# Turning the second group's frames on VectorE instead of TensorE, with K chunks by channel quarters

## The chip, the core and the metric

One core of a Trainium2 chip runs the whole kernel. The metric is the device time of one execution in microseconds (us). The engines are named as in the profile: PE is TensorE (matmuls; PEld its weight loads), DVE is VectorE, ACT is ScalarE, POOL is GpSimd and SP is the engine that issues most of the DMAs.

## What is computed

One layer of a streaming encoder for 2048 prompt frames and 32 sample frames of 1024 channels, all in fp32:

```python
hn = rmsnorm(h, g_mix)
proj = hn @ w_in                                  # 1024 -> 6 x 512
hA, bA, cA, zA, vB, zB = split(proj)              # 512 channels each
u = cA * hA
yA = bA * (causal conv, width 3, of u + bias) * silu(zA)
yB = (trailing means of vB over 2/4/8/16 frames, minus vB, @ pool_w, * scale) * silu(zB)
h = h + concat[yA, yB] @ w_out
h = h + (p @ w_ple) * sigmoid(rmsnorm(h, g_ple) @ w_ple_gate)
y = rmsnorm(h, g_final)                           # and the last u and v rows as states
```

The sum over the 1024 input channels of `hn @ w_in` may be taken in any order, if frames and weights use the same one. The change is about that order.

## The kernel before

**Exact products from parts.** An fp32 operand is held as two tiles, hi and lo. `split` (L81 and L84) makes them: ACT casts the hi part (L81) and VectorE subtracts it from the source to get lo (L84). A product runs as three passes over the pairs (hi·hi, hi·lo, lo·hi), each of four matmuls of 128x128 by 128x512 for a half of K, so 12 matmuls (`half_product`, L646).

**Seven products in place of eight.** The 2048 frames form four blocks of 512. `GROUPS` pairs them: group 0 has blocks 0 and 1, group 1 has blocks 2 and 3. The two blocks of a group and the two halves of the 1024 channels make a 2x2 matrix of frames, and two kinds of columns of w_in with the two halves make a 2x2 matrix of weights. One `pair` of projections takes seven products of combinations: of frames 11, 21, 22 and T1 to T4 (differences and sums of the four quarters of the matrix), of weights 11, 12, 22 and S1 to S4 (tiles `w_..._S`). `pair_weights` (L597) loads two raw weight tiles of 128x1024 (`raw_..a`, `raw_..b`) and builds the sums on VectorE (L606, L618). The results of a pair gather in three PSUM tiles x, y and z, which ACT and VectorE drain (L983, L986).

**Units.** A `Unit` (gi, j) is a group and a quarter j of 128 columns of each of the six projections. It runs three pairs, named zbv (zb and v), ch (c and h) and zab (za and b), between them the pooling matmuls `pm` (L870 to L872), the drain of pm (L874) and the convolution (four scalar-tensor-tensor steps on VectorE, L1103). The first unit of group 0 runs `plain`, without the seven products for the first ones. The order of units is group 0 with j from 0 to 3, then group 1.

**Frames of group 0.** Eight tiles of 128 frames x 1024 channels are loaded (`x_load`), their sum of squares is taken on ACT, rstd on POOL, and VectorE normalises them in place: block 0 with two 512-column instructions a tile (L700), block 1 with one of 1024 (L477). PE turns each 128x128 block through the identity (`turn`, L484, PSUM tiles `pt`) so that channels lie on partitions. `second_block` makes the combinations with block 1 during the plain unit. Of the seven pieces six fit; T4 is written to DRAM (`p_d["T4"]`) in four columns and read back as one piece of 2 MB into tile `B_T` (L941).

**Frames of group 1.** While group 0's units 1 to 3 run, the steps of `frame_sums` (L498) are called in small portions between the products (`aside`, at a pace of 13 steps in 18 calls). They go by columns: column c is the tile c of block 2 and the tile c of block 3, in the order 3, 0, 1, 2. A column is loaded (two DMAs of 512 KB), normalised on VectorE (L477), turned by PE (16 transposes into `pt_g`), combined on VectorE (`f_g`, L509), and each of its seven pieces is split into a staged tile and written to DRAM by POOL (`to_memory`, L546; names such as `11_1_3` for piece 11 of group 1, column 3, and `T` for the T's). At the end of group 0 `load_group(1)` (L556) loads seven pieces of 2 MB on POOL's queue (L560) and two raw weight tiles behind them.

**Buffers.** Frames, staged tiles and some weights share a pool of four tiles (`xin`), raw weights one of three (`raws`), split weights one of six. A staged tile is free again when its write has landed.

**Order.** Each engine has its own queue, and a scheduler fixes the order in it when the program is built; `tc.keep_in_program_order` (`in_turn`, `later`) pins single instructions to their place in the source. An engine never overtakes its own queue: an instruction that waits holds all behind it.

Of the kernel before, what the change touches and what calls it, by code (L numbers as in the profile page):

```python
# [36 lines left out]
def trunk(ctx, tc, x_p, x_s, c_conv, c_pool, p_p, p_s, g_mix, w_in, conv_w, conv_b, pool_w,  # L37
# [361 lines left out]
    with ExitStack() as s1:  # L399
# [78 lines left out]

        def turn(x, half, name, get=tbank, later=False):
# [92 lines left out]

        def raw_weight(kind, j, name, ring=raw_ring, queue=nc.sync):
# [4 lines left out]
            raw_loads.append(queue.dma_start(t, w_in[:, col:col + P].rearrange("(k p) n -> p k n", p=P)))  # L578
# [18 lines left out]
        def pair_weights(gi, ka, kb, j, name, ring, s_ring, ring_b, pin):  # L597
# [9 lines left out]
            if (ka, j) in kept:  # L607
# [5 lines left out]
                raw_loads.append(nc.sync.dma_start(rb[:, KH:], w_in[NH:, col:col + P].rearrange("(k p) n -> p k n", p=P)))  # L613
# [75 lines left out]
        B0 = {}  # L689
        ahead0 = [x_load(f"0_{c}", x_rows(0, c)) for c in range(4)]  # L690
# [3 lines left out]

        def first_normal(x):

            xt, m, r = x
            for half in range(2):
                h = xt[:m, half * NH:half * NH + NH]
                in_turn(nc.vector.scalar_tensor_tensor(h, h, r[:m], pg[half][:m], op0=ALU.mult, op1=ALU.mult))  # L700
# [76 lines left out]
        def second_block():  # L777

            spans = [(c, slice(c * P, c * P + P)) for c in range(4)]
            xs = []  # L780
            for c in range(4):
                x = x_stat(x_load(f"1_{c}", x_rows(1, c)))
                normal(x)
                xs.append(x)
                yield
            whole = []
            for c, cs in spans:
                x = xs[c]

                turned = x[0].rearrange("p (k t) -> p k t", k=KC)  # L790
# [7 lines left out]
            for c, cs in spans:  # L798
# [12 lines left out]
                to_memory(p_d["T4"], f"T4_0_{c}", t4, c * P)  # L811
                yield

        second = second_block()
# [21 lines left out]
        class Unit:  # L836
# [65 lines left out]
            def plain(self):  # L902
# [11 lines left out]

                wz, wv = weights("zb", j, f"zb{tag}"), weights("v", j, f"v{tag}")
# [24 lines left out]
                B0["T4"] = piece_of(seventh("B0_T4"), 0)  # L940
                nc.gpsimd.dma_start(B0["T4"].bitcast(F32), p_d["T4"])  # L941
# [261 lines left out]
        def next_columns(*cs):  # L1203

            ahead[cs[0]] = columns_in(1, cs[0])
# [636 lines left out]
```

## Time and profile before

| | |
|---|---|
| median of 3 runs | 919.31 us (918.29 to 919.38) |
| the profiled execution | 917.26 us |
| span of its trace | 915.5 us (1.76 us lie around it) |
| granted TensorE clock | 0.999 |
| PE busy | 895.3 us (98%), 4174 matmuls |
| VectorE busy | 702.6 us (77%) |
| ACT busy | 460.3 us (50%) |
| POOL busy | 151.6 us (17%) |

The units of group 0 end at about 277 us, the projections of group 1 run after them, and the output projection, gate and final norm fill the rest. A timeline row has the start, the duration, the engine, the line, the operation with output<-input, and in brackets the idle time before it with what ended it. A row of a line's summary has minimum, median and maximum duration in ns, and the first and the last start.

### The profile page before, as it was taken

How to read it: one execution, taken by the hardware profiler on the slowest of the kernel's cores; microseconds unless marked ns; L12 is line 12 of the kernel's file. 1: busy time of each engine (PE TensorE's matmuls, PEld its weight loads, DVE VectorE, ACT ScalarE, POOL GpSimd, SP SyncE). 2: the span in 40 equal slices, each digit the busy share in tenths (PEclk: the TensorE clock that was granted, in tenths of full speed). 3: DMA queues.
4: the chain of work that ended last, by engine and by line, in shares of the span. 5: the costliest groups of instructions: out<-in, count | busy, mean ns of one | idle time of the engine just before them, and what ended most of it. 6: DMA issues, size and time to landing. Idle time of an engine off the chain costs nothing.

```text
span 915.5 us, 12179 instructions
## 1 busy us (share of the span) xinstructions
PE 895.3 (98%) x4174; PEld 722.7 (79%) x4174; DVE 702.6 (77%) x1158; ACT 460.3 (50%) x834; POOL 151.6 (17%) x291
## 2 busy tenths in 40 slices
PE   8999999999999999999999999999999999999996
PEld 6787888878888877877778887888888788778885
DVE  6897899697894597856667679965576978897885
ACT  7743555555444344533344366544344865565554
POOL 2210121222122104100000020121111211120002
PEclk9999999999999999999999999999999999999999
DMA  8165386749499857577746485787677875575554
GB/s 275 53 186 184 115 239 182 219 147 301 122 313 427 244 161 228 191 231 247 244 132 215 146 310 206 259 235 273 226 258 291 287 256 173 184 234 187 183 187 171
DMA packets 113307, 199.56 MB, mean 218 GB/s; under 512 B 13190, under 2 KB 70062, under 8 KB 112221
## 3 DMA queue, kind: packets, MB, share of 16 engines
q1 hardware_dynamic: 91309, 124.72, 42.3%
q0 software_dynamic: 19488, 69.67, 22.5%
q10 hardware_dynamic: 2448, 4.39, 1.3%
q8 instruction: 33, 0.54, 0.2%
q14 instruction: 29, 0.24, 0.1%
HBM read 133.06 MB, written 65.67 MB: 217 GB/s over the span
## 4 chain that ended last, share of the span: by engine, by line
PE 65%; DMA 7%; issue 5%; DVE 2%; ACT 1%; POOL 1%; SPq 0%; POOLq 0%; DVEq 0%; ACTq 0%
PE x_g L185 9%; PE x_o L185 9%; PE x_zab L646 5%; PE z_g L185 5%; PE e L109 4%; PE x_zbv L646 4%; PE x_ch L646 4%; PE z_o L185 4%; DMA raw_zab_0b<-in_w_in_dram 4%; PE z_zab L646 2%; PE y_g L185 2%; PE y_o L185 2%; PE z_ch L646 2%; PE z_zbv L646 2%; DMA B<-p_d 2%
## 5 line engine op out<-in xcount | busy, mean ns | idle before, releaser
L646 PE MATMUL x_zab<-B,w_zab_S 128*128 128x512 f32 x192 | 46.9, 392 | 0.6 <-ACT V L983 0.4
L185 PE MATMUL z_o<-wo,y_S 128*128 128x512 f32 x192 | 47.4, 389 | 0.0
L185 PE MATMUL z_g<-wg,g_S 128*128 128x512 f32 x192 | 46.8, 391 | 0.0
L646 PE MATMUL z_zab<-B,w_zab_S 128*128 128x512 f32 x192 | 46.7, 390 | 0.0
L185 PE MATMUL x_o<-wo_T,y_S 128*128 128x512 f32 x192 | 46.1, 389 | 0.0
L185 PE MATMUL x_o<-wo,y 128*128 128x512 f32 x192 | 45.2, 389 | 0.0
L646 PEld LDWEIGHTS x_zab<-B,w_zab_S 128*128 128x128 f32 x192 | 35.7, 188 | 9.6 <-ACT V L983 0.8
L185 PEld LDWEIGHTS x_o<-wo,y 128*128 128x128 f32 x192 | 36.1, 188 | 7.7
L646 PEld LDWEIGHTS z_zab<-B,w_zab_S 128*128 128x128 f32 x192 | 35.8, 188 | 7.8 <-DVE w_zab_S L84 0.3
L185 PEld LDWEIGHTS z_o<-wo,y_S 128*128 128x128 f32 x192 | 36.0, 188 | 7.5
L646 PE MATMUL x_ch<-B,w_ch_S 128*128 128x512 f32 x168 | 41.9, 392 | 0.0
L185 PEld LDWEIGHTS x_o<-wo_T,y_S 128*128 128x128 f32 x192 | 36.0, 188 | 7.4
L646 PE MATMUL z_ch<-B,w_ch_S 128*128 128x512 f32 x168 | 40.5, 390 | 1.4 <-ACT U L983 1.4
L185 PEld LDWEIGHTS z_g<-wg,g_S 128*128 128x128 f32 x192 | 35.8, 188 | 7.5 <-ACT c_g L1566 0.2
L646 PE MATMUL x_zbv<-B,w_zbv_S 128*128 128x512 f32 x168 | 40.8, 392 | 0.6 <-ACT zs L983 0.6
L646 PE MATMUL z_zbv<-B,w_zbv_S 128*128 128x512 f32 x168 | 40.4, 390 | 0.0
L646 PEld LDWEIGHTS z_ch<-B,w_ch_S 128*128 128x128 f32 x168 | 31.5, 188 | 8.3 <-ACT U L983 1.8
L646 PEld LDWEIGHTS x_zbv<-B,w_zbv_S 128*128 128x128 f32 x168 | 31.3, 188 | 8.3 <-ACT zs L983 1.0
L646 PEld LDWEIGHTS x_ch<-B,w_ch_S 128*128 128x128 f32 x168 | 31.3, 188 | 7.3 <-issue 0.4
L646 PEld LDWEIGHTS z_zbv<-B,w_zbv_S 128*128 128x128 f32 x168 | 31.5, 188 | 6.5
L81 ACT CAST y_S<-y_fS 128x512 fp32r<-128x512 f32 x28 | 17.0, 620 | 27.2 <-PE x_o L185 11.5
L1316 DVE TENSOR_TENSOR c_o<-x_o,x 128x512 f32<-128x512 f32 x14 | 9.7, 690 | 21.9 <-PE x_o L185 21.8
(550 smaller groups left out, 2289.4 us busy)
## 6 DMA issues: line engine op xcount, KB each, us to landing
wn<-in_w_in_dram SPq DMA_DIRECT2D x24, 512.0 KB, 5.3
p_dT<-T POOLq DMA_DIRECT2D x16, 512.0 KB, 5.4
y<-y_d SPq DMA_DIRECT2D x16, 512.0 KB, 6.5
e<-e_d SPq DMA_DIRECT2D x15, 512.0 KB, 4.5
x<-in_x_prompt_dram SPq DMA_DIRECT2D x14, 512.0 KB, 5.2
B<-p_d POOLq DMA_DIRECT2D x3, 2048.0 KB, 15.7
B<-p_dT POOLq DMA_DIRECT2D x3, 2048.0 KB, 21.6
h_d<-x SPq DMA_DIRECT2D x12, 512.0 KB, 7.2
```

Source lines behind the costliest of these rows:

```text
L81: ins = nc.scalar.copy(hi, src)
L109: nc.tensor.matmul(ps, pps[:, a, k], wp[k][b][:, cs], start=k + q == 0, stop=k == 1 and q == 2)
L185: nc.tensor.matmul(ps[:n], lhs[:, k, a, :n], w[b][:, k], start=start and k + q == 0, stop=k == KH - 1 and q == 2, skip_group_check=True)
L646: nc.tensor.matmul(ps, lhs[:, k, x], b[:, k, y], start=start and k + q == 0, stop=stop and k == KH - 1 and q == 2, skip_group_check=True)
L1316: add = lambda o, a, b: nc.vector.tensor_tensor(o, a, b, op=ALU.add)
```

## The change

It takes the K dimension in another order, the same for frames and weights: chunk k, partition q·32 + r is channel q·256 + k·32 + r (before, channel k·128 + partition). In that order a turn needs only the transpose of 32x32 blocks, and VectorE has an instruction for that.

- **Frames of group 1**: a tile is loaded with four DMAs, each a quarter of the channels onto 32 partitions, so that VectorE's transpose of 32x32 blocks (128x1024 at once, in place) gives the turned tile. PE's 64 transposes, their PSUM tiles and two copies by ACT a column are gone. The sum of squares comes in eight squares of 128x256 a column and is put together across the four partition quarters on POOL; the normalisation is eight instructions of 128x256. The combinations are made in place in the two loaded tiles, which therefore hold two of the four tiles of `xin` until T4 is split; the seven pieces share the other two as staged tiles.
- **Weights of w_in**: every raw tile is loaded in that order, with four DMAs of 32 partitions in place of one of 128.
- **Frames of group 0**: still turned by PE. The normalisation writes a copy with the channels in the new order, as four instructions of 128x8x32 a tile.
- **T4 of group 0**: only the columns 0 to 2 go through DRAM (1.5 MB are read back, once column 2 is written), and the last column is split directly into `B_T`.

The core of the diff:

```diff
+        def normal_into(t, x, in_order=False, g=None):
+            xt, n, r = x
+            for q in range(4):
+                cs = slice(q * 2 * P, q * 2 * P + 2 * P)
+                o, h = t[:, :D].rearrange("p (k q c) -> p q k c", k=KC, q=4)[:, q], xt[:, cs].rearrange("p (k c) -> p k c", k=KC)
+                by = (g[q // 2][:, q % 2 * 2 * P:(q % 2 + 1) * 2 * P] if g else g_bc[:, cs]).rearrange("p (k c) -> p k c", k=KC)
+                ins = nc.vector.scalar_tensor_tensor(o, h, r, by, op0=ALU.mult, op1=ALU.mult)
+                if in_order:
+                    in_turn(ins)
+            return t, n, r
...
-            return [x_load(f"{tb}_{c}", x_rows(tb, c), queue) for tb in GROUPS[g]]
-        def four(xs, tag):
-            for half in range(2):
-                yield [turn(x, half, f"pt_{tag}_{i}_{half}", get=bank if half else tbank, later=True) for i, x in enumerate(xs)]
-        def frame_sums(xs, tag, dst):
-            xs = [x_stat(x, True) for x in xs]
+            xs = []
+            for tb in GROUPS[g]:
+                t = ring4(xin, f"xt_{tb}_{c}")
+                rows = x_rows(tb, c).rearrange("(g p) (q c) -> q p g c", p=32, q=4)
+                for q in range(4):
+                    queue.dma_start(t[q * 32:q * 32 + 32].rearrange("p (g c) -> p g c", g=4), rows[q])
+                xs.append(t)
+            return xs
+        def frame_sums(xs, tag, dst, norms):
+            for _ in range(3):
+                yield
+            g_q, part = norms[:, :2 * P], lambda i: norms[:, 2 * P + i * 8:2 * P + i * 8 + 8]
+            ssq, tot, ms, rr, other = (part(i) for i in range(5))
+            quarter = lambda i: slice(i * 32, i * 32 + 32)
+            for b, x in enumerate(xs):
+                for g in range(4):
+                    i = b * 4 + g
+                    tc.keep_in_program_order(nc.scalar.activation(junk[:, :2 * P], x[:, g * 2 * P:(g + 1) * 2 * P], AF.Square,
+                                                                  accum_out=ssq[:, i:i + 1]))
+                yield
+            first = quarter(0)
+            for q in range(1, 4):
+                nc.gpsimd.tensor_copy(other[first], ssq[quarter(q)])
+                nc.gpsimd.tensor_tensor(tot[first], other[first], (tot if q > 1 else ssq)[first], op=ALU.add)
+            nc.gpsimd.tensor_scalar(ms[first], tot[first], scalar1=1.0 / D, scalar2=EPS, op0=ALU.mult, op1=ALU.add)
+            nc.gpsimd.tensor_tensor(rr[first], ms[first], nhalf[first].to_broadcast([32, 8]), op=ALU.pow)
+            for q in range(1, 4):
+                nc.gpsimd.tensor_copy(rr[quarter(q)], rr[first])
+            for b, x in enumerate(xs):
+                for g in range(4):
+                    h = x[:, g * 2 * P:(g + 1) * 2 * P]
+                    nc.vector.scalar_tensor_tensor(h, h, rr[:, b * 4 + g:b * 4 + g + 1], g_q, op0=ALU.mult, op1=ALU.mult)
             yield
             for x in xs:
-                normal(x)
-                yield
-            f12, f1, f21 = (ftile(f"{c}_{tag}") for c in ("f12", "f1", "f21"))
+                nc.vector.transpose(x, x)
+            yield
+            u = [x.rearrange("p (g k t) -> p k g t", g=4, k=KC) for x in xs]
+            (p11, p21), (p12, p22) = ((v[:, :KH], v[:, KH:]) for v in u)
             sub = lambda o, x, y: nc.vector.tensor_tensor(o, x, y, op=ALU.subtract)
-            steps = four(xs, tag)
-            p11, p12 = next(steps)
-            nc.scalar.copy(f12, p12)
-            sub(f1, f12, p11)
             dst("11", p11)
-            yield
-            dst("T1", f1)
-            yield
-            p21, p22 = next(steps)
-            nc.scalar.copy(f21, p21)
-            sub(f1, p22, f1)
-            sub(f12, p22, f12)
+            sub(p11, p12, p11)
+            yield
+            dst("T1", p11)
+            sub(p11, p22, p11)
             yield
             dst("21", p21)
+            sub(p21, p21, p11)
+            yield
+            dst("T2", p11)
+            sub(p12, p22, p12)
             yield
             dst("22", p22)
-            yield
-            dst("T2", f1)
-            sub(f21, f21, f1)
-            yield
-            dst("T3", f12)
-            yield
-            dst("T4", f21)
-            yield
+            dst("T3", p12)
+            yield
+            dst("T4", p21)
...
             t = staged(name)
-            put(t, src, later)
+            whole = (lambda v: v.rearrange("p k (g t) -> p k g t", g=4)) if len(src.shape) == 4 else lambda v: v
+            split(whole(t[:, :, 0]), whole(t[:, :, 1]), src, later=later)
             nc.gpsimd.dma_start(mem[:, :, :, at:at + P], t.bitcast(F32))
...
+        def load_chunks(t, col, queue=nc.sync, ks=slice(0, KC)):
+            rows = w_in[:, col:col + P].rearrange("(q k c) n -> q c k n", q=4, k=KC)
+            for q in range(4):
+                raw_loads.append(queue.dma_start(t[q * 32:q * 32 + 32], rows[q][:, ks]))
         def raw_weight(kind, j, name, ring=raw_ring, queue=nc.sync):
             if name in raw_ahead:
                 return raw_ahead.pop(name)
             t = ring(f"raw_{name}")
             col = cols[kind] * WA + j * P
-            raw_loads.append(queue.dma_start(t, w_in[:, col:col + P].rearrange("(k p) n -> p k n", p=P)))
+            load_chunks(t, col, queue)
             return t
...
         def first_tile(c):
-            first_normal(first_x[c])
-            turned_x[c] = [turn(first_x[c], half, f"pt0_{c}_{half}", bank) for half in range(2)]
+            x = normal_into(room0 if c == 0 else ahead0[c - 1][0], first_x[c], True, pg)
+            turned_x[c] = [turn(x, half, f"pt0_{c}_{half}", bank) for half in range(2)]
...
                 op(t4, t4, part("21", 1), ALU.add)
-                to_memory(p_d["T4"], f"T4_0_{c}", t4, c * P)
+                if c < 3:
+                    to_memory(p_d["T4"], f"T4_0_{c}", t4, c * P)
+                else:
+                    B0["T4"] = piece_of(seventh("B0_T4"), 0)
+                    nc.gpsimd.dma_start(B0["T4"][:, :, :, :c * P].bitcast(F32), p_d["T4"][:, :, :, :c * P])
+                    put(B0["T4"][:, :, :, cs], t4)
                 yield
...
         def next_columns(*cs):
             ahead[cs[0]] = columns_in(1, cs[0])
+            norms = ftile("norms").rearrange("p k n -> p (k n)")
+            for q in range(4):
+                nc.gpsimd.dma_start(norms[q * 32:q * 32 + 32, :2 * P], g_mix[:, q * 2 * P:(q + 1) * 2 * P].partition_broadcast(32))
             for c, after in zip(cs, cs[1:] + (None,)):
                 dst = lambda q, src: to_memory(p_d[q], f"{q}_1_{c}", src, c * P, True)
-                for i, _ in enumerate(frame_sums(ahead.pop(c), f"g1_{c}", dst)):
-                    if i == 10 and after is not None:
-                        ahead[after] = columns_in(1, after, nc.gpsimd)
-                    yield
+                yield from frame_sums(ahead.pop(c), f"g1_{c}", dst, norms)
+                if after is not None:
+                    ahead[after] = columns_in(1, after, nc.gpsimd)
                 yield
```

More of the change, by code (lines that the diff above doesn't have):

```diff
@@ L612, in pair_weights @@
                 nc.sync.dma_start(rb[:, :KH], k3)
-                raw_loads.append(nc.sync.dma_start(rb[:, KH:], w_in[NH:, col:col + P].rearrange("(k p) n -> p k n", p=P)))
+                load_chunks(rb[:, KH:], col, ks=slice(KH, KC))
                 s3, a22 = rb[:, :KH], rb[:, KH:]
@@ L689, in trunk @@
         B0 = {}
+        room0 = bz.tile([P, D], F32, tag="t", name="room0")
         ahead0 = [x_load(f"0_{c}", x_rows(0, c)) for c in range(4)]
@@ L693, in in_turn @@
             tc.keep_in_program_order(ins)
[L695 to L700, printed above, removed]
         first_x, turned_x = [], {}
@@ L779, in second_block @@
             spans = [(c, slice(c * P, c * P + P)) for c in range(4)]
-            xs = []
+            xs, raw = [], []
             for c in range(4):
-                x = x_stat(x_load(f"1_{c}", x_rows(1, c)))
-                normal(x)
-                xs.append(x)
+                raw.append(x_stat(x_load(f"1_{c}", x_rows(1, c))))
+                xs.append(normal_into(raw[c - 1][0] if c else room1[0], raw[c]))
                 yield
@@ L788, in second_block @@
                 x = xs[c]
-                turned = x[0].rearrange("p (k t) -> p k t", k=KC)
+                turned = (xs[c][0] if c else raw[3][0]).rearrange("p (k t) -> p k t", k=KC)
                 for half, q in enumerate(("12", "22")):
@@ L810, in second_block @@
                 op(t4, t4, part("21", 1), ALU.add)
-                to_memory(p_d["T4"], f"T4_0_{c}", t4, c * P)
+                if c < 3:
[4 more added lines that the diff above has]
+                    put(B0["T4"][:, :, :, cs], t4)
                 yield
+        room1 = []
         second = second_block()
@@ L913, in product_of @@
                     return ps
+                room1.append(U)
                 wz, wv = weights("zb", j, f"zb{tag}"), weights("v", j, f"v{tag}")
@@ L939, in plain @@
                     next(second)
-                B0["T4"] = piece_of(seventh("B0_T4"), 0)
-                nc.gpsimd.dma_start(B0["T4"].bitcast(F32), p_d["T4"])
                 p_d["T4"] = tc.dram_tile([P, KH, 2, NB], F32, name="p_dT4b")
```

## The prediction

> **What bounds the kernel now.** I read the busy table first, then the waits of TensorE, then the timeline around each operation that the change takes away.
>
> ```profile
> span 915.5 us, 12179 instructions
> PE 895.3 (98%) x4174; PEld 722.7 (79%) x4174; DVE 702.6 (77%) x1158; ACT 460.3 (50%) x834; POOL 151.6 (17%) x291
> PE x_zab L646 <- DMA B_T<-p_dT: 2.3, 1, 2.3
> PE pt_g L484 <- DVE xt L477: 0.7, 1, 0.7
> PE x_zab L646 <- DVE w_zab_S L84: 0.2, 1, 0.2
> ```
>
> TensorE (PE) works 98% of the span, so work taken from it is time, and every new wait of its fixed queue is time too. The three waits (us in total, times, longest) are the only ones that the change can remove; all are small. The change acts between the start and about 280 us, so that stretch is what counts, not the average:
>
> ```profile
> 80.00:280.00 200.00, 195.24 (x887) 160.22 (x886) 169.92 (x284) 99.00 (x178) 41.34 (x59) 1.00 0.69 216
> ```
>
> The columns are the stretch, its length, the busy time of PE, PEld, DVE, ACT and POOL, the granted clock, DMA share and GB/s. There VectorE (DVE) has 169.92 of 200 us, 85% where the mean of the span is 77%. PE has 4.76 us of idle in those 200, among them the 2.3 of B_T. VectorE also makes the lo halves of the weights that PE needs, so its queue order decides as much as its load.
>
> **What is removed.** The 64 identity transposes of group 1:
>
> ```profile
> L484 PE MATMUL pt_g<-ident,xt 128*128 128x128 f32 x64 | 8.5, 273 | 0.7 <-DVE xt L477 0.7
> 148.75 1.03 PE L484 MATMUL pt_g<-ident,xt 128*128 128x128 f32 x8
> 149.54 2.98 PE L646 MATMUL x_zab<-B_T,w_zab 128*128 128x512 f32 x12
> 152.36 1.03 PE L484 MATMUL pt_g<-ident,xt 128*128 128x128 f32 x8
> 153.15 2.98 PE L646 MATMUL x_zbv<-B,w_zbv 128*128 128x512 f32 x12
> 258.20 2.88 PE L646 MATMUL x_zab<-B,w_zab 128*128 128x512 f32 x12
> 260.92 2.88 PE L646 MATMUL y_zab<-B,w_zab 128*128 128x512 f32 x12
> ```
>
> Busy time counts the overlap of neighbours, so I go by starts. Eight transposes hold the queue for 149.54 − 148.75 = 0.79 us, and the product of 12 behind them takes 152.36 − 149.54 = 2.82. A plain product takes 2.72 from start to start (260.92 − 258.20). So a set of eight costs 0.79 + 0.10 = 0.89, eight sets 7.1 us, not the 8.5 of busy time. With the wait before pt_g (0.7) that is −7.8. The wait for B_T should go as well: only three quarters of the piece are still loaded, earlier, and the last is written by ACT and VectorE. In the changed order its lo half is two rows behind a weight that I place at 77.2 below, and the product starts at:
>
> ```profile
> 88.11 2.98 PE L646 MATMUL x_zab<-B_T,w_zab 128*128 128x512 f32 x12 [2.28 <-DMA B_T<-p_dT]
> ```
>
> That is ten us of slack: −2.3. Removed in all: −10.1 us.
>
> **What VectorE gets.** The costs of its forms:
>
> ```profile
> L477 DVE SCALAR_TENSOR_TENSOR xt<-xt,rstd_x,g_bc x12: 1279/1285/1287, 23.1 to 229.7; 128x1024 f32<-128x1024 f32 x12
> L700 DVE SCALAR_TENSOR_TENSOR xt<-xt,rstd_x,gm x8: 740/743/748, 7.0 to 15.6; 128x512 f32<-128x512 f32 x8
> L1553 DVE STREAM_TRANSPOSE hn<-hn x8: 1235/1237/1241, 709.0 to 882.0; 128x1024 f32<-128x1024 f32 x8
> L84 DVE TENSOR_TENSOR T<-f_g,T x16: 682/684/693, 109.8 to 262.4; 128x512 fp32r<-128x512 f32 x16
> 133.68 2.74 DVE L1103 SCALAR_TENSOR_TENSOR c_s<-U,vec,c_s 128x512 f32<-128x512 f32 x4
> 125.40 1.29 DVE L84 TENSOR_TENSOR T<-f_g,T 128x512 fp32r<-128x512 f32 x2
> 23.08 1.29 DVE L477 SCALAR_TENSOR_TENSOR xt<-xt,rstd_x,g_bc 128x1024 f32<-128x1024 f32 x1 [0.72 <-POOL rstd_x L77]
> ```
>
> No 256-column form is in the trace. 1285 and 743 ns differ by 1.06 ns a column, which gives 0.47 us for 256 columns alone; in a row each instruction starts some 0.08 before its forerunner's end (1.29 for two of 0.684), so I take 0.39, between the 0.32 of pure proportion and 0.47. A column of group 1 then gets eight of 0.39 (3.1) for two of 1.21 (2.4), and two turns of 1.15: +3.0 us a column, +12 over four, while the subtractions and lo halves remain. VectorE goes from 169.9 to about 182 of the 191 us that the stretch would have without the removed PE time: 95%. That is no bound yet, but it leaves nothing with which to catch up after a wait. [...]
>
> In the first group the permuted copies are four pieces per tile for one of 1024 (block 1) or two of 512 (block 0). The transposes of a tile wait for all four, so the start gets about 4 × 0.39 − 2 × 0.67 = 0.2 us, and the first tile waits for pieces in a row instead of starting after half: +0.4 (0.2 to 0.8). In block 1 VectorE's 0.35 us a tile is hidden behind idle like the 0.72 us before each 1024-column normalisation; if that cover is gone it is 1.4.
>
> **Where PE must wait for VectorE.** The built order of the changed kernel fixes VectorE's queue, so I walked it with these durations (0.60 for a 512-column tensor-tensor, 0.68 for a scalar-tensor-tensor).
>
> Unit 0: the lo half of the second zab weight sum stands behind the step that drains y_zab and one T4 step.
>
> ```profile
> 68.75 2.88 PE L646 MATMUL x_zab<-B,w_zab 128*128 128x512 f32 x12
> 72.40 2.14 PEld L646 LDWEIGHTS y_zab<-B,w_zab 128*128 128x128 f32 x10 [0.28 <-DVE w_zab L84]
> 74.80 2.88 PE L646 MATMUL x_zab<-B,w_zab_S 128*128 128x512 f32 x12
> 75.33 0.68 DVE L986 TENSOR_TENSOR V<-y_zab,V 128x512 f32<-128x512 f32 x1
> ```
>
> From the end of the h product at 68.8 the fourteen rows that end with it (one of them waits for y_zab, at 74.6) take until about 77.2. PE could start its lo matmuls at about 75.1: +2.1, less the 0.3 that PE loses to a lo half here now, so +1.8 (0 to 3).
>
> Unit 1 (column 3) is the worst place. Now the lo half of w_zab is done long before PE is there:
>
> ```profile
> 121.06 0.68 DVE L84 TENSOR_TENSOR w_zab<-raw_zab_1a,w_zab 128x512 fp32r<-128x512 f32 x1
> 128.31 2.88 PE L646 MATMUL x_ch<-B_T,w_ch 128*128 128x512 f32 x12
> 131.03 0.39 PE L870 MATMUL pm<-pp,pw 128*128 128x512 f32 x1
> 131.71 2.88 PE L646 MATMUL x_zab<-B,w_zab 128*128 128x512 f32 x12
> ```
>
> In the changed order it stands behind the step that needs the last x_ch product, behind the drain of pm, four convolution steps and five tensor-tensors (two lo halves of frames, the weight sums). With X the end of x_ch: the drain of pm can end at X + 1.5, four convolutions 2.7, five rows 3.0, so the weight is ready at X + 7.3. PE has 0.7 of pm and 0.9 of hi-only matmuls: it waits at least 5.5 (up to 6.5 if the staged tiles' writes, for which two of these rows wait, are late). Behind it the ACT drain of x_zab stands behind the hi casts of T2 and T3, and pm of the next unit behind a late lo half: +1.5 (0 to 2.5). Together +7.0. For units 2 and 3 (columns 0 and 1) the same walk leaves each weight ready 5 to 13 us early: nothing.
>
> The switch to group 1 (column 2): now the first piece of the column is written and loaded long before group 1 begins.
>
> ```profile
> 240.73 0.93 POOL L546 DMA_DIRECT2D p_d<-11_1_2_2237  x1 [11.05 <-DVE 11_1_2_2237 L84]
> 264.52 1.29 POOL L560 DMA_DIRECT2D B<-p_d  x2
> 277.24 2.88 PE L646 MATMUL x_zbv<-B,w_zbv 128*128 128x512 f32 x12
> 270.00:280.00 10.00, 10.00 (x46) 8.29 (x45) 9.42 (x18) 2.94 (x5) 3.41 (x7) 1.00 1.01 426
> p_dT<-T POOLq DMA_DIRECT2D x16, 512.0 KB, 5.4
> B_T<-p_dT POOLq DMA_DIRECT2D x1, 2048.0 KB, 9.7
> ```
>
> Call Z the start of the zab products of unit 3, 258.20 now; group 1 begins 19.0 later. In the changed order VectorE normalises the column only at Z + 2 to 5.1, does two convolutions (7.2), turns both tiles (9.5) and makes the lo half of 11 (10.1). Two staged tiles serve all seven pieces, so the lo half of 21 waits for the landing of 11 (5.4 by the row): 16.2. On POOL the load of piece 11 stands behind the write of 21, so it is issued at Z + 17.1. Two MB take 4.9 us at 426 GB/s and 9.7 as B_T did. So PE would wait 3.0 to 7.7, and from VectorE's order alone (the first zbv lo half stands three rows behind the drain of the last x_zab) it waits 1.0. I take the middle, +5.5 (1 to 9, the upper end with the cast of w_ch on ACT, which waits behind two casts of T). Later pieces come every 4.9 us, and PE uses one in 2 × 2.72 = 5.44.
>
> **Loads.** Four weight loads of 128 KB replace each one of 512:
>
> ```profile
> hn<-h_d SPq DMA_DIRECT2D x33, 128.0 KB, 3.0
> hn<-h_d SPq DMA_DIRECT2D x8, 512.0 KB, 4.8
> ```
>
> A quarter takes 3.0 us to land beside 4.8 for the whole; even one after another four take 12 us, while a pair of weights serves seven pieces of 5.44, 38 us. I cost it at nothing; its cover is the lead with which raw tiles are fetched, and it would be a few us at most where the raw tile is already late.
>
> The sum: −10.1 + 0.4 + 1.8 + 7.0 + 5.5 = +4.6 us. The profiled execution is 917.26 (span 915.5 and 1.76 around it), so it becomes 921.9; the median, 919.31, is 2.05 higher, and stands at 923.9.
>
> **The rivals.** A: PE's removed work wins. The walk takes every row of VectorE at its modelled place; if the waits come out near their lower ends (0.2 + 0 + 4 + 2.5, unit 1 shorter because PE, itself later, gives VectorE time to get ahead), the sum is −3.4: 916 (914 to 918). For it: 98% of PE, and all three waits that PE shows now are short, so an order on this chip tends to leave little. Against it: the 7.3 us behind X is a chain of one engine and cannot be shortened by lead.
>
> B: VectorE becomes the bound. From the point where its waits for staged tiles (5.4 us a landing, only two tiles) use up the 9 us it has left in the stretch, each further us is paid: three more landings half hidden, some +8 on my sum: 932. For it: 95%. Against it: units 2 and 3 have leads of 5 us and more.
>
> C: the quarter loads arrive late. [...] No row here shows four quarters issued for one weight in this stretch. The mechanism in rows of this kernel: four landings of 3.0 in turn instead of 4.8, 7.2 us later for the first weight of each of the later units; where one is exposed it costs +4 on my sum: 928.
>
> D: the change doesn't do what it says for T4: the three-quarter load is still late and the 2.3 stay: 926.
>
> **How the numbers follow.** Forecast 0.47, A 0.27, B 0.16, C 0.06, D 0.04. A measurement of this kernel can tell about 0.2%, 1.8 us, from no change. Faster by more: A nearly whole and the lower tail of the forecast's bounds (unit 1 at 4, switch at 1), 0.28; within: 0.08; slower: 0.64. The range takes A in from 913.5 and B up to 932.
>
> **What would show it.** In the changed profile: no pt_g, no wait for B_T; a wait of 4 to 7 us before the first x_zab of unit 1, ended by VectorE's lo half of w_zab; 2 us at the second zab sum of unit 0; a wait of 3 to 8 us before the first x_zbv of group 1, ended by the load of B; VectorE busy about 182 us between 80 and the switch. It is wrong if PE passes unit 1 or the switch with under 2 us, or if PE idles in units 2 and 3.

## The result

The changed kernel takes 991.51 us (median of 4 runs, 988.05 to 993.49) against 918.80 for the kernel before (918.13 to 919.38): a ratio of 1.0774, 95% interval 1.0745 to 1.0803. It is slower, as forecast, but by 72.7 us where 4.6 were forecast, far outside the range. The profiled execution is 993.49 us with a span of 991.7. Its page:

```profile
span 991.7 us, 12474 instructions
...
PE 908.4 (92%) x4110; PEld 727.9 (73%) x4110; DVE 718.0 (72%) x1210; ACT 462.4 (47%) x874; POOL 170.4 (17%) x346
...
PEclk9999989999997589999999999999999999999999
DMA  8375258394839931496676629687777886566544
```

Two things grew on TensorE. It idles 991.7 − 908.4 = 83.3 us instead of 20.2: +63.1. And it is busy 13.1 us longer with 64 transposes less, which were 8.5 us of busy time: its other work takes 21.6 us more. PEclk, the granted clock in tenths in 40 slices, shows why: it falls to 7 and 5 about a third of the way along, where it was 9 throughout before:

```profile
PEclk9999999999999999999999999999999999999999
```

In finer windows of the changed kernel, nine stretches between 79 and 404 us have a granted clock of 0.50. TensorE is busy for 37.5 us in them; at half the clock, half of that, 18.8 us, is lost. That is most of the 21.6; where the rest comes from is not settled. 63.1 + 21.6 − 8.5 = 76.2 us, the difference of the two spans.

The waits of TensorE, and its products at the three places that the prediction named or missed:

```profile
PE x_ch L682 <- ACT w_ch L81: 36.6, 1, 36.6
PE x_zbv L682 <- DMA B<-p_d: 7.8, 1, 7.8
PE x_zab L682 <- DVE w_zab L84: 5.6, 1, 5.6
PE x_zab L682 <- DVE w_zab_S L84: 4.3, 2, 2.3
PE pm L906 <- DVE pp L84: 3.2, 2, 3.0
PE pm L905 <- ACT pp L81: 2.9, 2, 2.2
PE x_zbv L682 <- ACT zs L1017: 2.8, 2, 2.3
PE z_zab L682 <- ACT U L1017: 2.7, 1, 2.7
```

```profile
79.11 4.14 PE L682 MATMUL x_zab<-B,w_zab_S 128*128 128x512 f32 x10 [2.27 <-DVE w_zab_S L84]
...
121.35 0.79 PE L906 MATMUL pm<-pp,pw 128*128 128x512 f32 x1 [2.97 <-DVE pp L84]
...
145.73 4.63 PE L682 MATMUL x_zab<-B,w_zab 128*128 128x512 f32 x10 [5.60 <-DVE w_zab L84]
...
310.11 5.33 PE L682 MATMUL x_zbv<-B,w_zbv 128*128 128x512 f32 x12 [7.79 <-DMA B<-p_d]
352.09 4.87 PE L682 MATMUL x_ch<-B,w_ch 128*128 128x512 f32 x12 [36.65 <-ACT w_ch L81]
```

The first, third and fourth of these rows are the waits that the prediction placed. The last, 36.65 us, is half of the whole loss and is in no term of its sum. Each row also shows a second loss: twelve matmuls take 2.88 us when TensorE has been busy (258.20 in the trace of before), 4.9 to 5.3 behind a long wait, and even ten take 4.1 to 4.6.

How far each start lies behind that of the kernel before, from the timelines, beside what the prediction's terms add up to at the same place:

| place | before | after | behind by | by the prediction |
|---|---|---|---|---|
| first zab of unit 0 | 68.75 | 70.15 | 1.4 | 0.4 |
| first zab of unit 1 | 131.71 | 139.07 | 7.4 | −1.9 |
| first zbv of unit 2 | 153.15 | 166.59 | 13.4 | 3.3 |
| first zab of unit 3 | 258.20 | 278.38 | 20.2 | −0.9 |
| first zbv of group 1 | 277.24 | 310.11 | 32.9 | 4.6 |
| first ch of group 1 | 279.96 | 352.09 | 72.1 | 4.6 |
| end of span | 915.5 | 991.7 | 76.2 | 4.6 |

Where the 36.65 us come from: first the load's issue on SP's queue in the kernel before, then in the changed kernel, and what that issue waited for by the chain of work that ended last.

```profile
259.67 0.38 SPq L578 DMA_DIRECT2D raw_ch_0a<-in_w_in_dram  x1
```

```profile
314.29 1.98 SPq L607 DMA_DIRECT2D raw_ch_0a<-in_w_in_dram  x4
```

```profile
305.12 9.02 DMA p_d<-22_1_2_2628
```

Then the timelines of ACT and POOL:

```profile
314.08 0.62 ACT L81 CAST T<-xt 128x512 fp32r<-128x512 f32 x1 [0.76 <-DVE T L84]
...
351.42 0.62 ACT L81 CAST w_ch<-raw_ch_0a 128x512 fp32r<-128x512 f32 x1 [29.30 <-DMA raw_ch_0a<-in_w_in_dram]
```

```profile
317.07 1.18 POOL L591 DMA_DIRECT2D B<-p_dT  x2
...
324.57 0.53 POOL L591 DMA_DIRECT2D B_T<-p_dT4b  x1 [1.55 <-DMA p_dT4b<-T]
```

The raw weights of the first ch pair of group 1 take their two tiles from `xin` (in `seven`, `spare_ring` where `both` is true), the pool in which frames now stay until T4 is split. The load is issued at 314.29, when the last two pieces of column 2 are only being split; in the kernel before it was issued at 259.67. The chain names, as what the issue waited for, the write of piece 22 from its staged tile. That write took 9.02 us, where the like of it (p_dT<-T) took 5.4 before; the first 2 MB loads, issued from 299.71 on, ran beside it (the DMA share was 1.01 in these 9.02 us) and likely slowed it, which no run isolates. Now the weight load, too, runs beside the pieces of 2 MB. ACT gets the tile at 351.42, about when the last of these lands: T4's load, issued at 324.57, took 27.3 us.

Of the runs below, two of the four of e6 took over 1.5% longer than its fastest and are not in its ratio.

### The profile page after: what moved, and what is told of

The parts are those of the page before. It is cut to its first block, busy times and chain, and to the rows that moved or that the text cites. A ratio compares the mean times of both kernels' runs of the same rounds, so it can differ in the third digit from the quotient of the medians.

```text
span 991.7 us, 12474 instructions
## 1 busy us (share of the span) xinstructions
PE 908.4 (92%) x4110; PEld 727.9 (73%) x4110; DVE 718.0 (72%) x1210; ACT 462.4 (47%) x874; POOL 170.4 (17%) x346
## 3 DMA queue, kind: packets, MB, share of 16 engines
q0 software_dynamic: 20080, 68.75, 21.3%
## 4 chain that ended last, share of the span: by engine, by line
PE 60%; DMA 12%; issue 12%; DVE 10%; POOL 3%; ACT 2%; SPq 1%; POOLq 0%; DVEq 0%; ACTq 0%
PE x_g L185 9%; PE x_o L185 7%; PE x_zab L682 6%; PE z_g L185 4%; PE x_ch L682 4%; PE x_zbv L682 4%; DMA raw_ch_0a<-in_w_in_dram 4%; PE z_o L185 3%; PE z_zab L682 3%; PE z_ch L682 2%; PE z_zbv L682 2%; PE y_g L185 2%; PE e L109 2%; PE y_o L185 2%; DVE f L826 1%
## 5 line engine op out<-in xcount | busy, mean ns | idle before, releaser
L682 PE MATMUL x_ch<-B,w_ch 128*128 128x512 f32 x84 | 22.3, 419 | 36.6 <-ACT w_ch L81 36.6
L682 PE MATMUL x_zab<-B,w_zab_S 128*128 128x512 f32 x192 | 49.7, 408 | 4.3 <-DVE w_zab_S L84 4.3
L682 PE MATMUL z_zab<-B,w_zab_S 128*128 128x512 f32 x192 | 49.2, 405 | 2.7 <-ACT U L1017 2.7
L682 PEld LDWEIGHTS x_ch<-B,w_ch 128*128 128x128 f32 x84 | 16.9, 204 | 41.4 <-ACT w_ch L81 37.2
L682 PEld LDWEIGHTS z_zab<-B,w_zab_S 128*128 128x128 f32 x192 | 37.9, 198 | 11.4 <-ACT U L1017 3.1
L682 PE MATMUL x_ch<-B,w_ch_S 128*128 128x512 f32 x168 | 44.7, 413 | 0.2 <-ACT c_s L1017 0.2
L682 PEld LDWEIGHTS x_ch<-B,w_ch_S 128*128 128x128 f32 x168 | 33.3, 200 | 8.7 <-ACT c_s L1017 0.6
```

What stands on the lines that cost most here:

```text
L682: nc.tensor.matmul(ps, lhs[:, k, x], b[:, k, y], start=start and k + q == 0, stop=stop and k == KH - 1 and q == 2, skip_group_check=True)
```

## The experiments

Each ratio is to the kernel before, timed beside it, with a 95% interval. Where two experiments are compared in us, it is the difference of their ratios times 918.8.

**e1: ch weights ahead of the pieces.** In `load_group`:

```diff
-            for q in NAMES:
+            for q in NAMES[:2]:
+                nc.gpsimd.dma_start(B[q].bitcast(F32), p_d[q])
+            for kind, part in (("c", "a"), ("h", "b")):
+                raw_ahead[f"ch_{g}_0{part}"] = raw_weight(kind, 0, f"ch_{g}_0{part}", spare_ring, nc.gpsimd)
+            for q in NAMES[2:]:
                 nc.gpsimd.dma_start(B[q].bitcast(F32), p_d[q])
```

> The changed kernel, with the two raw tiles of the first ch pair of group 1 loaded on the same queue as the pieces and ahead of pieces T2 to T4. Theory (the 36.6 us wait is a weight load of 512-byte rows that is issued late, because its buffer is held by column 2's frames, and then shares the DMA engines with 14 MB of pieces until these are done): the load lands within 10 us of its issue, the wait before the first x_ch of group 1 falls to under 10 us, and the whole to 955 to 968 us. Rival (the DMA engines are full in any order, so the wait only moves to piece T2 or T1): the waits between the switch and 30 us behind it still add up to over 35 us and the time stays over 980.

Measured: 967.71 us, 1.0519 (1.0489 to 1.0548), 23 us less than the changed kernel. The load is issued at 315.52, 1.2 us later than without the edit, and lands 6.6 us after its issue; the wait falls to 10.5. So the place among the loads is what made its landing late; the edit changes both the queue (SP's to POOL's) and the order there, and this run does not tell the two apart. The time is in the expected range, the wait half a microsecond over the expected bound: the tile is still freed late.

```profile
315.52 2.40 POOL L611 DMA_DIRECT2D raw_ch_0a<-in_w_in_dram  x4
```

```profile
324.06 0.62 ACT L81 CAST w_ch<-raw_ch_0a 128x512 fp32r<-128x512 f32 x1 [3.42 <-DMA raw_ch_0a<-in_w_in_dram]
```

**e2: quarter loads alone**, on the kernel before, same K order:

```diff
-            raw_loads.append(queue.dma_start(t, w_in[:, col:col + P].rearrange("(k p) n -> p k n", p=P)))
+            rows = w_in[:, col:col + P].rearrange("(k q c) n -> q c k n", q=4, k=KC)
+            for q in range(4):
+                raw_loads.append(queue.dma_start(t[q * 32:q * 32 + 32], rows[q]))
```

> The kernel before, with each raw weight load of w_in cut into four DMAs of 32 partitions, K order unchanged. Theory (the quarter loads are hidden): 918 to 921 us. Rival C of the prediction (they arrive late): over 924 us, with PE waits for weights from the second unit on.

Measured: 927.9 us, 1.0086 (1.0061 to 1.0112), +7.9 us: rival C's size, though in another place. Of 7.2 us by which the first ch of group 1's third unit is late (429.20 against 422.04), 5.4 arise between the first zab of its first unit (+2.9) and the next zbv (+8.3). There the quarters of `raw_zab_0b` on POOL's queue are issued one by one, the last three each when a piece has landed:

```profile
295.17 0.58 POOL L576 DMA_DIRECT2D raw_zab_0b<-in_w_in_dram  x1 [5.26 <-DMA y_d<-c_s]
300.41 0.58 POOL L576 DMA_DIRECT2D raw_zab_0b<-in_w_in_dram  x1 [4.66 <-DMA B<-p_dT]
305.35 0.58 POOL L576 DMA_DIRECT2D raw_zab_0b<-in_w_in_dram  x1 [4.36 <-DMA B<-p_d]
312.00 0.58 POOL L576 DMA_DIRECT2D raw_zab_0b<-in_w_in_dram  x1 [6.06 <-DMA B_T<-p_dT4b]
```

Each of these three waits ends with the landing of the DMA that stands eight issues earlier on this queue (the fifth, sixth and seventh pieces). With four issues a tile the eight reach back into the pieces; the kernel before issued the whole tile at 279.70. But this is not shown to be the way of the loss. VectorE first reads `raw_zab_0b` at 323.43, behind another of its operations and 6.6 us after the tile had landed (316.86), so nothing waits for it. What TensorE waits for are the split weights, whose casts and lo halves now come later in the queues of ACT and VectorE, mixed with other work. Here are ACT's casts, first in e2, then before:

```profile
317.51 0.61 ACT L81 CAST w_zab<-raw_zab_0a 128x512 fp32r<-128x512 f32 x1
```

```profile
312.26 1.12 ACT L81 CAST w_zab<-raw_zab_0a 128x512 fp32r<-128x512 f32 x2
```

So the loss sits in the order that the built program fixed for these engines. Why it fixed another one is open: `raw_zab_0a` also lands later, at 314.5 against 309.0.

**e4: the T4 part alone**, on the kernel before, as in the diff above.

> The kernel before with only the T4 part of the change. Theory: the 2.3 us wait for B_T goes and nothing takes its place, 916 to 917.5 us. Rival D: the wait stays, 918 to 920 us.

Measured: 915.6 us (8 runs), 0.9946 (0.9930 to 0.9962). The wait is gone, TensorE passes the place without idle:

```profile
82.38 2.88 PE L646 MATMUL z_zab<-B,w_zab_S 128*128 128x512 f32 x12
85.10 2.88 PE L646 MATMUL x_zab<-B_T,w_zab 128*128 128x512 f32 x12
```

The gain, 3.5 to 6.4 us by the interval, is more than the 2.3 of the wait; its one profile is only 0.4 us shorter than the first of before, with a new wait of 2.6 us (z_o for c_o) later on. Where the rest comes from is not settled. This version beats both kernels.

**e5: frame steps at every product.**

```diff
-                    aside = at_pace(next_columns(3, 0, 1, 2), 13, 18)
+                    aside = at_pace(next_columns(3, 0, 1, 2), 1, 1)
```

> The changed kernel with the steps of the second group's frames called at every product (1 in 1) instead of 13 in 18, so that column 2 is done before the last third of unit 3. Theory (lateness of column 2 makes both the wait for piece 11 and the wait for the ch weights): the wait for B<-p_d at the switch goes, the wait before the first x_ch of group 1 falls under 15 us, 940 to 962 us. Rival (VectorE is too full to do the columns sooner, so the same time is lost in units 1 to 3): over 975 us.

Measured: 991.88 us, 1.0789 (1.0757 to 1.0822): no change, and the expectation of 940 to 962 missed. The rival's time came, over 975. The wait for piece 11 goes, but the wait for ch stays at 33.5 us although its load now starts at 300.85, 13 us sooner. The pieces moved forward with it.

```profile
300.85 20.32 SPq L607 DMA_DIRECT2D raw_ch_0a<-in_w_in_dram  x4
```

The four issues alone take 20.32 us, the third and fourth 9.6 and 9.5. The two quarters whose landing is recorded took 45.5 and 36.0 us; the load is there at about 347, when the last piece lands too. So it is not only a late issue: beside the pieces the weight load was slow in both places, at 314 (35.62 us in the chain) and at 301 (36.0 and more).

**e6: e1 and e5 together.**

> The changed kernel with both edits of e1 (ch weights ahead of the pieces) and e5 (frame steps at every product). Theory (a 512-byte-row load beside the 2 MB pieces lands only with the last of these, whenever it is issued; the pace removes the wait for piece 11): the 33.5 us wait of e5 falls under 8 us, 945 to 960 us. Rival (the earlier columns cost as much in units 1 to 3 as they save): 965 us and over.

Measured: 1.0417 (1.0373 to 1.0461), from runs of 958.17 and 962.37 us. The load of ch lands 5.5 us after its issue, and the waits for it and for piece 11 are gone. The expected fall to 960 just came; but other waits have grown against e1 (13.2 us in all for w_zab_S, the longest 6.4, where e1 has 4.5; 5.4 for c_s where e1 has none), so the rival is half right.

**e7: waits of e1 filled with identity transposes.**

```diff
+                for _ in range({(0, 1, "za"): 45, (1, 0, "zb"): 65, (1, 0, "c"): 85}.get((self.gi, self.j, ka), 0)):
+                    tc.keep_in_program_order(nc.tensor.transpose(X[:, :P], ident, ident))
                 half_product(X, upper or make("11"), B["11"], True)
```

> e1 with identity transposes put on TensorE into three of its waits (45 before the first x_zab of unit 1, 65 before the first x_zbv and 85 before the first x_ch of group 1, each about 0.1 us), all shorter than the wait they stand in. Theory (the products behind a wait are slow because TensorE was idle, which lowers its granted clock, and each wait costs 1.7 to 2.9 us more than itself): the first product behind each of the three goes from 4.4 to 5.5 us back to 2.9, and the time falls by 4 to 9 us, to 958 to 964. Rival (the slow products have another cause, or the added work only adds): 967 us or more, products as slow as before.

Measured: 966.58 us, 1.0486 (1.0456 to 1.0515), 3 us less than e1 by the ratios, 1 by the medians, and the intervals overlap: no gain clear of noise. The products behind the two waits that were filled almost wholly take 2.58 and 3.02 us (4.63 and 5.33 in the changed kernel); a wait of the same run that was left open, and the ch wait of which 3.59 us remained, still have slow ones (5.49 and 4.73):

```profile
144.97 2.58 PE L686 MATMUL x_zab<-B,w_zab 128*128 128x512 f32 x10 [0.64 <-DVE w_zab L84]
...
291.57 5.49 PE L686 MATMUL z_zab<-B,w_zab_S 128*128 128x512 f32 x12 [3.59 <-ACT U L1021]
...
307.30 3.02 PE L686 MATMUL x_zbv<-B,w_zbv 128*128 128x512 f32 x12 [0.17 <-DMA B<-p_d]
...
323.19 4.73 PE L686 MATMUL x_ch<-B,w_ch 128*128 128x512 f32 x12 [3.59 <-ACT w_ch L81]
```

So idleness is what slowed the products behind these waits. But the 4 to 9 us that I expected did not clearly come. The likely reason, which no run isolates: time saved on TensorE ahead of a wait for a transfer or for VectorE mostly lengthens that wait. The first x_ch of group 1 starts at 323.19 where it starts at 324.73 in e1.

**e8: group 1's frames not turned** (on e1): the two turns and six of eight normalisations of each column are left out.

> e1 with group 1's frames neither turned nor, but for the first quarter, normalised: the two turns and six of eight normalisations of each column are left out, some 4.6 us of VectorE a column. If VectorE's load is what makes the waits of units 1 to 3 and at the switch: those in units 1 to 3 all but go and the time is 945 us or less. If the order of the queues and the landings of staged tiles make them: most stay, 955 to 966 us.

Measured: 958.98 us, 1.0409 (1.0380 to 1.0438), 10 us under e1 and in the second of the expected ranges. The wait of unit 1 for w_zab goes and that for piece 11 falls to 2.1 us, but 3.2 and 2.1 stay before pm, 3.9 for w_zab_S, and the ch wait doubles to 21.0 us. The ch load explains the last: issued at 301.69, 0.5 us behind a piece of 2 MB, it took 12.5 us to land. 17 us less of VectorE's work (699.9 us busy against 716.9) brought about 10: its load is a part, and most of e1's loss stays without it.

**e9: staged tiles from the pool of the split weights** (on e1):

```diff
-            return xin.tile([P, KH, 2, P], F32R, tag="t", name=name)
+            return (wtile if "_1_" in name and "pps" not in name else lambda name: xin.tile([P, KH, 2, P], F32R, tag="t", name=name))(name)
```

> e1 with the staged tiles of group 1 taken from the pool of the split weights (six tiles) instead of the pool that the frames hold, so that two columns of frames fit and a piece seldom waits for the landing of the one before. Theory (held tiles and landings make column 2 late): the waits for piece 11 and for ch at the switch both fall under 4 us, 935 to 955 us. Rival (VectorE's order is what makes it late): both waits stay over 5 us, 960 us and over.

Measured: 1008.0 us, 1.0935 (1.0906 to 1.0964): a miss. No wait for a piece is left among those of TensorE over 1.6 us, but now TensorE waits for weights: in all 8.5 us of y_zab for w_zab, 7.3 of x_zab for w_zab_S, 7.1 of x_zbv for w_zbv. Split weights and staged pieces now share six tiles, so it is likely that the weights wait for the pieces' tiles; the profile does not show it, as only one of ACT's waits ahead of a weight's cast, 0.93 us long, is ended by a landing.

**e11: ACT's squares and casts of frames unpinned** (on e1): `keep_in_program_order` around the squares and the `True` in `to_memory(..., True)` taken out.

> e1 with ACT's squares and hi casts of group 1's frames no longer pinned to their place in the source. Theory (pinned, they stand ahead of ACT's drains of PSUM, and the waits of PE for ACT's zs, U and pp come from that): these waits, about 9 us in e1, fall under 4 and the time to 955 to 963 us. Rival (VectorE's queue is behind them): 965 to 971 us.

Measured: 962.06 us, 1.0465 (1.0432 to 1.0497), 5 us under e1, just clear of noise, and in the expected range. TensorE's waits for zs and U fall from 3.0 and 3.6 to 1.9 and 0.9; those for pp and w_zab_S remain, so the waits for ACT do not fall under 4 as expected. Those for piece 11 and w_zab go, while the one for ch grows from 10.5 to 18.5: its load, issued at 297.80, 0.7 us behind a piece of 2 MB, took 15.0 us to land. The pins are a part of it.

**e12: group 1 turned by TensorE again**, all else as changed: `columns_in`, `frame_sums` and `next_columns` of the kernel before, with

```diff
-            for x in xs:
-                normal(x)
+            for i, x in enumerate(xs):
+                xs[i] = normal_into(ring4(xin, f"turned_{tag}_{i}"), x)
```

> The changed kernel with group 1's frames loaded whole and turned by TensorE as before (after a permuting normalisation into another tile), the quarter loads of weights, the new K order and the T4 part kept. Theory (turning in place on VectorE, with frames held until T4, is what costs; the rest is the 7.9 us of quarter loads less the 5 us of T4 and 1.4 at the start): 920 to 930 us, no wait over 10 us at the switch. Rival (the new loads of the weights are what makes the ch load late): a wait of over 20 us before the first x_ch of group 1 and over 945 us.

Measured: 930.54 us, 1.0119 (1.0075 to 1.0162). This splits the loss: 0.0655 of the 0.0774, about 60 us, belong to the new way of making group 1's frames, and the quarter loads, the permuted copies and T4 together cost about 11. The new way is a bundle: loads in four parts, POOL's statistics, pinned squares and casts, turning and combining in place on VectorE, and the tiles held for it. The 60 us are net of the transposes that this run gives back to TensorE, and no run splits the bundle further. No wait is over 2.7 us. With the same quarter loads the ch weights are issued at 265.4, ahead of the pieces (from 268.6), and land in 3.4 us: quarter loads alone do not make them late.

**e13: without the three empty steps ahead of each column** (on e1).

> e1 without the three empty steps ahead of each column. Theory (column 2 comes too late for the switch): each column comes three steps sooner, the wait for piece 11 falls under 3 us and that for ch under 6, 950 to 962 us. Rival (the loads of the frames then come too late, as these empty steps cover them): the waits move to units 1 to 3 and the time stays at 965 us or over.

Measured: 989.81 us, 1.0767 (1.0728 to 1.0806): the time is the rival's, and in part the place: TensorE waits 13.4 us in unit 2 (for w_zbv_S) and 7.6 in unit 3 (for w_zab). That frames' loads come late, the rival's reason, is not seen; ahead of the 13.4, ACT's casts of the weights stand behind pinned casts that wait for staged tiles:

```profile
175.23 0.62 ACT L81 CAST T<-xt 128x512 fp32r<-128x512 f32 x1 [4.04 <-DMA p_dT<-T]
```

The largest wait is neither's. The ch load is in time here, but `raw_zbv_0b`, issued on SP's queue at 301.79 in four quarters, now meets the pieces, and VectorE stands still for it until 347.04; TensorE waits 24.2 us behind that.

```profile
347.04 0.69 DVE L656 TENSOR_TENSOR s_zbv<-raw_zbv_0b 128x512 f32<-128x512 f32 x1 [33.17 <-DMA raw_zbv_0b<-in_w_in_dram]
```

It is the same loss as the ch load's in the changed kernel, with another tile.

**e14: e1, e5 and e11 together.**

> The three edits that each helped, together: ch weights ahead of the pieces (e1), frame steps at every product (e6) and ACT's squares and casts unpinned (e11). If the waits have separate causes the savings add up: 940 to 955 us, no wait over 8 us. If the column's work on VectorE is the common cause, they overlap: 956 us or over. In neither case is it under 930 us, where the same change with TensorE's turns stood.

Measured: 963.49 us, 1.0453 (1.0414 to 1.0492). The savings overlap, as in the second expectation, but not for its reason alone. The largest waits are now 13.2 us of y_ch for w_ch and 6.6 of y_zab for w_zab, both on VectorE's lo halves. The lo half of w_ch is late because VectorE stands for a raw weight again, loaded on SP's queue from 285.44 on beside the pieces; the lo half follows at 321.61:

```profile
321.00 0.69 DVE L657 TENSOR_TENSOR s_zbv<-raw_zbv_0b 128x512 f32<-128x512 f32 x1 [25.21 <-DMA raw_zbv_0b<-in_w_in_dram]
```

It is the loss of e13 once more: moving the ch load alone leaves the next raw tile beside the pieces.

## Why the prediction was wrong, point by point

**The step that failed: buffers and loads.** The prediction costed the loads at nothing, covered by "the lead with which raw tiles are fetched". It never asked which tiles the raw weights take. Of the tiles in the pool that the frames now hold, it charged only the staged ones; the ch weights were in the same pool. So the load was issued 55 us later, among the pieces, and TensorE stood 36.65 us for it. In the changed kernel and in e5 it landed with the end of the pieces (351.4 beside 351.8, and about 347 in both cases), at whichever of the two places it was issued. The size was to be had from the trace of before, by its DMA issues from 262 to 300 us:

```profile
raw_zab_0b<-in_w_in_dram POOLq DMA_DIRECT2D x1, 512.0 KB, 32.1
raw_zbv_1a<-in_w_in_dram SPq DMA_DIRECT2D x1, 512.0 KB, 24.6
```

A whole weight tile took 24.6 us on SP's queue beside the pieces, and 32.1 on POOL's queue behind them, where it takes 5.3 elsewhere (the wn loads). There it was hidden, as nobody needed it yet. The two rows that the prediction took, 3.0 and 4.8 us (the hn loads), come from the stretch of 693 to 878 us, where the DMA share was 0.65 against 1.03 from 262 to 300, and were the wrong ones for this place. A queue of its own did not keep a weight load quick beside POOL's pieces: SP's took 36 us and more in e5, and in e13 VectorE stood 33.17 us for one. Why the weight loads lost so much time beside the pieces, no run here tells.

**The clock had no term.** Each stall was charged its own length. Behind the nine of 2.04 us and more between 79 and 404 us TensorE also ran slowly for 3.3 to 6.1 us, 1.7 to 2.9 us more each, 18.8 us over the nine stretches at half the clock. The windows of the changed kernel (length, busy times of PE, PEld, DVE, ACT, POOL, then the granted clock):

```profile
80.00:82.00 2.00, 2.00 (x6) 1.54 (x6) 2.00 (x5) 0.00 (x0) 0.00 (x0) 0.50 0.58 181
...
320.00:350.00 30.00, 0.00 (x0) 0.00 (x0) 0.00 (x0) 0.58 (x1) 3.35 (x6) 0.50 1.03 393
356.00:360.00 4.00, 4.00 (x19) 3.23 (x19) 1.48 (x3) 1.62 (x3) 0.00 (x0) 0.99 0.00 0
```

The granted clock was 0.50 behind 2.27 us of idle at 79 us (a few matmuls with gaps lie ahead of it), behind 2.35 at 243 us and behind 2.04 at 399 us; behind the wait of 2.28 at 88 us of before it was 1.00 (from 88 to 92 us). In e2 the ten products behind one of only 1.58 us, again with gaps ahead, took 4.16 us, where ten took 2.43 at 81.76 of the same run. So these runs give no length from which on a wait costs the clock.

**Right: the named waits of units 0 and 1.** Unit 0: 2.27 us measured, 2.1 walked. Unit 1: 5.60, 5.5 walked (the rows behind X add up to 7.2, not 7.3, and the lo half came at X + 7.1). A queue order with durations of the same forms gave these two waits to within half a microsecond.

**In part luck: the switch.** 7.79 us measured, walked as 3.0 to 7.7 with 5.5 taken. The wait, its place and its releaser are right, but two steps were late by about as much:

```profile
284.97 3.26 DVE L540 SCALAR_TENSOR_TENSOR xt<-xt,norms 128x256 f32<-128x256 f32 x8 [4.11 <-POOL norms L536]
```

```profile
299.71 0.63 POOL L591 DMA_DIRECT2D B<-p_d  x1
```

With Z = 278.38, VectorE normalised at Z + 6.6 instead of Z + 2, as it waited for POOL's statistics, and piece 11's load was issued at Z + 21.3 instead of Z + 17.1. TensorE itself came at Z + 23.9 instead of Z + 19.0, held up by a wait for U (2.72 us) and slow products. Each error is 4 to 5 us and they cancel.

**Wrong: "units 2 and 3: nothing", and pm.** The prediction itself named idling in units 2 and 3 as a sign that it is wrong, and TensorE idles there. Its walk checked weights only. It left out POOL's statistics and ACT's pinned casts, on which VectorE's and ACT's queues now stand still:

```profile
119.42 1.28 DVE L540 SCALAR_TENSOR_TENSOR xt<-xt,norms 128x256 f32<-128x256 f32 x3 [3.26 <-POOL norms L536]
120.61 0.69 DVE L84 TENSOR_TENSOR pp<-pl,pp 128x512 fp32r<-128x512 f32 x1
```

```profile
291.40 0.62 ACT L81 CAST 11_1_2_2520<-xt 128x512 fp32r<-128x512 f32 x1 [4.08 <-DVE xt L543]
...
293.71 0.63 ACT L988 ACTIVATE V<-V 128x512 f32<-128x512 f32 x1 [1.68 <-DVE V L1020]
294.24 0.57 ACT L1017 COPY U<-z_zab 128x512 f32<-128x512 f32 x1
```

The lo half of pp stands behind normalisations that wait 3.26 us for POOL, and TensorE's pm waits 2.97 for it. In all VectorE waited 14.8 us for these statistics, in four waits. ACT waits 4.08 us for the turn with the cast of 11, then 1.68 for V, which VectorE makes behind the same turn, and the drain of z_zab behind it comes too late for TensorE (2.72 us). e11 took part of the latter away.

**Wrong: rival B.** VectorE is no bound: between 80 us and the switch at 310.11 it was busy 180.07 us, close to the 182 forecast, but that is 78% of the stretch, since it waits too. e8 took 17 us of its work away and got about 10.

**Rivals A and D.** A went the wrong way. It also leaned on a misreading: the view of before lists nine more waits of TensorE, up to 2.3 us long, not three. D is out, as the wait for B_T is gone.

**Right, but small.** The turns on TensorE and the wait for B_T are gone. The 256-column form takes 0.481 us alone and 0.41 in a row (0.47 and 0.39 estimated), the turn 1.224 (1.237). The start lost 1.4 instead of 0.4, about half of it also in e2.

**Rival C** was real in size, +7.9 us instead of +4, but its mechanism, four landings in turn, is not shown there; how the loss of e2 comes about is open. I had put it at 0.06 in the belief that the cover was deep everywhere.

## What to carry to other kernels

When a change keeps a buffer longer, list everything else that takes tiles from its pool, and ask beside which transfers those loads will then run; take their duration from a row in that company, not from a quiet one. Walk every queue for head-of-line waits (an operation at the head holding up those behind it: 3.26 us on VectorE's queue and 4.08 on ACT's here), the statistics and pinned casts included, not just the engine that makes the weights. And count in that the products behind a TensorE wait may run at half the clock (0.50 behind nine waits of 2.04 us and more in the changed kernel, but 1.00 behind one of 2.28 in the kernel before), 1.7 to 2.9 us more each time here; a later wait for another engine may swallow part of that, the likely reason why e7 gained only 1 to 3 us.

## What the runs showed of the hardware that I had not expected

The quarters of a 512 KB weight load landed 3.4 us after their issue ahead of the pieces (e12), 6.6 in the same queue ahead of most of them (e1), 12.5 and 15.0 right behind a piece just issued (e8, e11), and two of them 36.0 and 45.5 beside them from another queue (e5). Behind waits of 2.04 us and more the granted clock was 0.50 in the changed kernel, behind one of 2.28 it was 1.00 in the kernel before, and behind one of 1.58 with gaps ahead of it ten products took 4.16 us (e2). And work of no use on TensorE during a wait (e7) brought the products behind it from 4.6 and 5.3 us to 2.6 and 3.0, while the time as a whole moved by 1 to 3 us, not clear of noise.
